# Conditioning of the second norm's scale: nine blocks in three bf16 parts, seven of them split on GpSimd

## The chip, the core and the metric

The kernel runs on one core of a Trainium2 chip. Five engines matter here. TensorE (PE in the profile; its weight loads are PEld) multiplies matrices. VectorE (DVE), ScalarE (ACT) and GpSimd (POOL) do the element work. SyncE (SP) issues most of the DMAs; the POOL queue issues some. The metric is the device time of one execution in microseconds.

## The reference, cut to what matters

One step of a one-layer decoder runs over 288 tokens: 256 of a prompt and 8 samples of 4 tokens. Nine conditioning vectors, one for the prompt and one per sample, give six modulation rows through one large weight:

```python
mod = (jax.nn.silu(c) @ w_ada + b_ada).reshape(n, N_MOD, 1, D_MODEL)
sh_m, sc_m, gt_m, sh_f, sc_f, gt_f = [mod[:, i] for i in range(N_MOD)]
...
h2 = _rms(x, g_ffn) * (1 + sc_f) + sh_f
gate, up = jnp.split(h2 @ w_ffn_in, 2, axis=-1)
x = x + gt_f * ((jax.nn.silu(gate) * up) @ w_ffn_out)
```

The change is about `sc_f`, the scale of the second norm: nine rows of 2048 values that must be there before `h2` is made. Everything is float32.

## The kernel before

**The main stream.** All large products run as steps on PE. A step loads a 1 MB block of weights by one SP DMA into one of five `raw` buffers. ACT copies each segment of 512 columns to a rounded upper part (`hi`), DVE subtracts to get the rest (`lo`), and PE multiplies three times for every 128 columns (L575 to L577: upper by upper, upper by rest, rest by upper), each with 288 columns moving. `hi` and `lo` have four buffers each (SPB), so ACT may begin the next segment only when PE has finished the one four segments back. This order of ACT, DVE and PE repeats through the whole kernel.

**The list of steps around the change** is `d0 + wo`, numbered from 0. Steps 0 to 35 are projections (`wD`), 36 to 43 the product `pa`, 44 to 51 the product `pb`, 52 to 67 the product `wo`, which adds to `x` and collects the squares for the second norm. Each of the steps 36 to 67 holds 48 matmuls. `beside[i]` lists what is put in after step i. Then come four blocks `fk`, which begin the FFN with the not yet normed `x` times the scale, and the long FFN stream (`ff`).

**The conditioning.** `w_ada` is cut into units; unit `a4` is `sc_f`, unit `a5` is `gt_f`. Each has 16 blocks of 128 rows by four groups of 512 columns. The nine columns of silu(c) lie in `cs`, padded to 32, and are the stationary operand; the weights move. The four groups of 512 run on four groups of 32 array columns (`tile_position`). There are two forms:

- Class `Ada` (L423) multiplies the float32 block as it is loaded. All 16 blocks of `a4` use it, eight after step 47 and eight after step 57. In each eight, four blocks arrive as eight pieces of 256 columns in the shared `slot` pool (`apart`, by the function `eight`), the rest in `raw`. All are loaded by SP.
- Class `Thirds` is used by all 16 blocks of `a5`. ACT casts the block to bf16 (`cast`), DVE subtracts twice in place (`cut`), and so the block becomes three bf16 parts whose sum is the float32 value. PE multiplies each part with a stationary operand that holds silu(c) in three bf16 parts of nine columns (`csr`), and `fin` adds the three. A block that is `lent` sits in 12 tiles of the `slot` pool and is handled in pieces of 256 columns, else in the pool `thirds` in pieces of 1024. The POOL queue loads both kinds (L594, L599). For `a5`, `prepared` places loads, casts, cuts and products by a written plan.

After the last block of `a4`, `tail` copies the sum out of PSUM, PE transposes it, and DVE adds the bias into `mod`. The sink of `wo` block 8 makes `gm2` from it, and from there on `scaled` (L312) makes two of the sixteen operands of `fk` per step, with small GpSimd operations.

**Order.** DVE, ACT and SP are no longer held to program order in this part. PE is held by `S["pe"]` up to step 52, where `strict` is switched off. A planner places the instructions of each engine by its own costs. Two blocks are split early and kept: `fk[3]` in the pool `short` and the first `ff` block in `slot`, at steps 60 and 61. `change` closes the pool `short` and opens `thirds` in its place, after `fk`.

Of the kernel before, what the change touches and what calls it, by code (L numbers as in the profile page):

```python
# [89 lines left out]
def _body(tc, nc, d, pc, pw, pslot, pshort, reopen, ptmp, pps):  # L90
    ids = [0]

    def nm(s):
        ids[0] += 1
        return f"{s}_{ids[0]}"
# [16 lines left out]
    def behind(i):  # L112
        return tc.issue_after(i.ins) if i is not None else ExitStack()
# [17 lines left out]
    V, A, G, PE, SY = Pinned(nc.vector), Pinned(nc.scalar), nc.gpsimd, nc.tensor, Pinned(nc.sync)  # L131
# [34 lines left out]
    cs = cs9[:, NC:].rearrange("p (k i) -> p k i", i=32)  # L166
# [7 lines left out]
    def part16(a, i):  # L174
        return a.bitcast(BF16).rearrange("p (n b) -> p b n", b=2)[:, i, :]
# [1 line left out]
    def change():  # L177
        S["thirds"] = reopen()

    def thirds_columns():  # L180
        c = tmp(16 * NC)
        cv = c.rearrange("p (k i) -> p k i", i=NC)
        r = S["csr"] = pc.tile([P, 16, 32], BF16, tag="cs", name="csr", padded_shape=[P, 16, 64])
        V.tensor_scalar(cv, ctt, 0.5, None, ALU.mult)
        for i in range(3):
            ri = r[:, :, NC * i : NC * i + NC]
            V.tensor_copy(ri, cv)
            if i < 2:
                V.tensor_tensor(cv, cv, ri, ALU.subtract)
        V.tensor_scalar(  # L190
            r[:, :, 3 * NC :], ones[:, : 32 - 3 * NC].unsqueeze(1).to_broadcast([P, 16, 32 - 3 * NC]), 0.0, None, ALU.mult
        )
# [104 lines left out]
    def in_order(i):  # L297
        if S["strict"]:
            S["pe"] = i
        return i  # L300
# [79 lines left out]
    class Step:  # L380
        defer = False
        after, lead = None, 0
        raw = None
        parts = None
# [104 lines left out]
    class Blk(Step):  # L489
# [55 lines left out]
                self.low()  # L545

        def keep(self):
            for c in range(0, self.nk * self.nm * P if not self.parts else 0, 256):
                raw, (hi, lo) = self.raw[:, c : c + 256], [slot(F32R, (P, 256), self.kept == "short") for _ in range(2)]
                with behind(S["high"]):  # L550
                    A.copy(hi, raw)
                V.tensor_tensor(lo, raw, hi.bitcast(F32), ALU.subtract)
                self.parts += [(hi[:, i : i + P], lo[:, i : i + P]) for i in (0, P)]
# [28 lines left out]

    class Thirds(Ada):
        lent = False

        def load(self):
            src = d[self.name][self.blk]
            self.ks = 1
            if self.lent:
                self.words = [slot(shape=(P, 256)) for _ in range(8)]  # L590
                tops = [slot(shape=(P, 256)).bitcast(BF16) for _ in range(4)]
                self.tops = [tops[i // 2][:, 256 * (i % 2) : 256 * (i % 2) + 256] for i in range(8)]
                for i, w in enumerate(self.words):
                    G.dma_start(w, src[:, 256 * i : 256 * i + 256])  # L594
                return
            raw = S["thirds"].tile([P, 2048], F32, tag="word", name=nm("word"))
            top = S["thirds"].tile([P, 2048], BF16, tag="top", name=nm("top"))
            self.words, self.tops = ([t[:, 1024 * h : 1024 * h + 1024] for h in range(2)] for t in (raw, top))
            G.dma_start(raw, src)  # L599

        def pieces(self):
            n = 2 if self.lent else 1
# [7 lines left out]
        def cut(self, piece):  # L610
            for i in piece:
                r = self.words[i]
                with behind(S["low"]):
                    V.tensor_tensor(r, r, self.tops[i], ALU.subtract)
                V.tensor_tensor(part16(r, 0), r, part16(r, 1), ALU.subtract)

        def run(self):
            if self.blk == 0:
                Ada.cur[self.name] = pps.tile([P, 512], F32, tag="ada", name=nm("ada"), bufs=1)
            acc = Ada.cur[self.name]  # L620
            n = 256 if self.lent else 512
            for p in range(3):
                parts = self.tops if p == 0 else [part16(w, 2 - p) for w in self.words]
                for h in range(512 // n):
                    for j in range(4):
                        at = 512 * j + n * h
                        w, o = parts[at // (2048 // len(parts))], at % (2048 // len(parts))
                        with behind(S.get("pe")):
                            self.last = in_order(
                                PE.matmul(  # L630
                                    acc[32 * j : 32 * j + 32, n * h : n * h + n],
                                    S["csr"][:, self.blk, :],
                                    w[:, o : o + n],
                                    start=self.blk == 0 and p == 0,
                                    stop=self.blk == 15 and p == 2,
                                    tile_position=(0, 32 * j),
                                    skip_group_check=True,
                                )
                            )
            self.words = self.tops = None  # L640
            if self.blk == 15:
                self.tail()
# [70 lines left out]

    def ada(name):
        u = units[name]
        return [(Thirds if name == "a5" else Ada)(u, b) for b in range(16 // u[3])]


    S = {"strict": True}
# [517 lines left out]
            done = max(done, want)  # L1237
        return out

    def prepared(main, unit, plan):  # L1240
        out = {i: [] for i in range(-1, len(main))}
        blks = iter(unit)
        for last, parts in plan:
            for lent, begin_, (p0, p1) in parts:
                u = next(blks)
                u.lent = lent
                out[begin_].append(Do(u.load))
                n = 4 if lent else 2
                for i in range(n):
                    k = p0 + (p1 - p0) * i // n  # L1250
                    out[k].append(Do(lambda u=u, i=i: u.cast(u.pieces()[i])))
                    out[k + 1].append(Do(lambda u=u, i=i: u.cut(u.pieces()[i])))
                out[last].append(Do(u.run))
        return sum(([s] + out[i] for i, s in enumerate(main)), out[-1])

    rh1 = h1.__getitem__
# [63 lines left out]
    steps = [Do(silu), Do(lambda: warm(10)), *aA[:2], Do(lambda: warm(1, aA[1].last)), aA[2]]  # L1320
# [15 lines left out]
    def wD(m0, m1):  # L1336
        return [Blk("wD", i, rh1, sinkD) for i in range(m0 // 2, m1 // 2)]

    d0 = wD(32, 40)
# [7 lines left out]
    wo = [Blk("wo", i, mg.__getitem__, sink_wo) for i in range(16)]  # L1347
    a2, a3, a4 = ada("a2"), ada("a3"), ada("a4")
    a2[-1].defer = True

    def late(unit):
        unit[-1].tail = unit[-1].out
        return [Do(lambda: unit[-1].fin(chained))]

    def eight(blks):
        for b in blks[1:5]:
            b.apart = True
        return blks


    def ffin(q):
        fi = [Blk("fi", i - 4, h2.__getitem__, lambda j, ps: sink_fi(j + 4, ps)) for i in range(max(4, 22 * q), 22 * q + 22)]
# [3 lines left out]
    fk[0].defer = fk[1].defer = True  # L1366
    ff = ffin(0)
    early = [fk[3], ff[0]]
    early[0].kept, early[1].kept = "short", "long"
    beside = {}  # L1370
    for i in range(8):
        beside[5 * i + 2] = []
# [1 line left out]
    for i, (a, b) in ((7, (0, 5)), (12, (5, 10)), (17, (10, 15)), (22, (15, 20)), (27, (20, 25)), (37, (25, 32))):  # L1374
        for u in aa[a + 1 : b - 3]:
            u.apart = True
        beside[i] += aa[a:b]
    beside[42], beside[47], beside[57] = [], eight(a4[:8]), eight(a4[8:])
    for i in range(4):
        beside[5 * i + 7].append(Do(v_transpose(i)))  # L1380
        beside[5 * i + 27].append(Do(spatial(i)))
# [1 line left out]
    beside[22] += [Do(s_transpose), Do(sg_load)]  # L1383
    beside[5] = [Do(v_squares)]
    beside[42][:0] = late(a3) + [Do(half_gt)]
    for i, s in enumerate(d0 + wo):
        if s is wo[0]:
            steps.append(Do(lambda: S.update(strict=False, pe=None)))
        if s in (wo[8], wo[9]):
            steps.append(Do(early[s is wo[9]].split))  # L1390
        steps += [s] + beside.pop(i, [])
    def ffout(q):
        return [Blk(f"f{q}", i, act.__getitem__, sink_fo(q)) for i in range(16)]
# [3 lines left out]
    a5 = ada("a5")  # L1397
# [1 line left out]
        nxt = ffin(q + 1)  # L1399
        ff += nxt[:2] + ffout(q) + nxt[2:]  # L1400
    out3 = ffout(3)
    steps.append(Do(change))
    plan = [
# [4 lines left out]
    ]  # L1408
    rest = prepared(ff, a5, plan)
    rest.insert(rest.index(ff[5]), Do(thirds_columns))  # L1410
    steps += rest + out3[:2] + [Do(join15)] + out3[2:] + [Do(finish)]

    AHEAD = RAW
# [4 lines left out]
    order = list(stream)  # L1418
    for s in [s for s in stream if isinstance(s, Ada) and s.apart]:
        i = order.index(s)  # L1420
        order.remove(s)
        order.insert(i - 6 + (s.blk % 8 if s in a4 else 1), s)
    for s, b in zip(early, (wo[7], wo[8])):
        order.remove(s)
        order.insert(order.index(b), s)
    for s in order:
# [14 lines left out]
    blks = [s for s in stream if isinstance(s, Blk)]  # L1441
    nxt, cur = 0, 0
    for s in steps:
# [3 lines left out]
        i = pos[id(s)]  # L1447
# [141 lines left out]
```

## Time and profile before

| | |
|---|---|
| three runs | 1513.66, 1515.87, 1517.86 us; median 1515.87 |
| the profiled execution | 1513.66 us, its span 1511.9 us |
| PE, PEld | busy 1504.7 and 1449.6 us |
| DVE, ACT, POOL | busy 1060.9, 776.5 and 176.6 us |
| granted TensorE clock | 0.999 |

The span is what the profile covers; 1.8 us lie around it. Times in a timeline are microseconds from the span's start. The pieces of one matmul row overlap, so the pace of PE is read from the starts of successive matmuls, not from their durations.

### The profile page before, as it was taken

To read this page: it belongs to the slowest core of one execution; us is meant where nothing else is said; L and a number is where in the kernel's file an instruction comes from. 1 tells how busy PE (TensorE), PEld (TensorE's weight loads), DVE (VectorE), ACT (ScalarE), POOL (GpSimd) and SP (SyncE) were. 2 spreads that over 40 slices of the span, in tenths; PEclk is the share of its full clock that TensorE was granted. 3 is DMA by queue.
4 is the path that set the end of the run, shared out by engine and by line. 5 is a ranking of instruction groups with operands and counts; after the bars stand their busy time and mean duration, and the time that the engine had idled before them with its cause. 6 is when DMAs were issued, how large, how long until landed. Compare 5 with 4: busy or idle time off the path is not lost.

```text
span 1511.9 us, 32334 instructions
## 1 busy us (share of the span) xinstructions
PE 1504.7 (100%) x12734; PEld 1449.6 (96%) x12734; DVE 1060.9 (70%) x2099; ACT 776.5 (51%) x1487; POOL 176.6 (12%) x353
## 2 busy tenths in 40 slices
PE   9999999999999999999999999999999999999998
PEld 8898999998899898989999999999999999999998
DVE  6786677978666576667878666666666567675586
ACT  5443354743345444457655455455545454454465
POOL 2555410000030000002500101100010100100000
PEclk9999999999999999999999999999999999999999
DMA  9977876578888778875654657564575745754452
GB/s 390 357 282 301 344 272 219 197 285 313 328 321 311 261 258 299 272 278 204 225 190 163 218 189 244 205 215 142 180 248 183 251 136 178 243 186 157 146 176 98
DMA packets 75689, 357.75 MB, mean 237 GB/s; under 512 B 9248, under 2 KB 28512, under 8 KB 46352
## 3 DMA queue, kind: packets, MB, share of 16 engines
q1 hardware_dynamic: 70384, 337.02, 62.4%
q0 software_dynamic: 5008, 18.59, 3.5%
q8 instruction: 99, 1.62, 0.4%
q14 instruction: 54, 0.44, 0.1%
q10 hardware_dynamic: 144, 0.07, 0.0%
HBM read 352.56 MB, written 3.09 MB: 235 GB/s over the span
## 4 chain that ended last, share of the span: by engine, by line
PE 100%; DVEq 0%; DVE 0%; issue 0%
PE pm L575 30%; PE pm L577 30%; PE pm L576 30%; PE ada L423 5%; PE ada L630 1%; PE px L304 1%; PE px L310 0%; PE pm L690 0%; PE pm L692 0%; PE pm L691 0%; PE pm L674 0%; PE px L733 0%; PE px L692 0%; PE px L691 0%; PE px L690 0%; PE pm L304 0%
## 5 line engine op out<-in xcount | busy, mean ns | idle before, releaser
L575 PE MATMUL pm<-s,hi 128*128 128x288 f32 (+1 forms) x3688 | 1058.1, 287 | 0.0
L577 PE MATMUL pm<-s,lo 128*128 128x288 f32 (+1 forms) x3688 | 1055.0, 286 | 0.0
L576 PE MATMUL pm<-s,hi 128*128 128x288 f32 (+1 forms) x3688 | 1054.9, 286 | 0.0
L124 ACT CAST hi<-raw 128x512 fp32r<-128x512 f32 (+2 forms) x956 | 578.4, 606 | 633.7 <-PE pm L576 547.1
L124 DVE TENSOR_TENSOR lo<-raw,hi 128x512 fp32r<-128x512 f32 (+2 forms) x959 | 657.2, 691 | 333.5 <-ACT hi L124 310.8
L575 PEld LDWEIGHTS pm<-s,hi 128*128 128x128 f32 x3688 | 697.0, 189 | 10.8 <-issue 8.9
L576 PEld LDWEIGHTS pm<-s,hi 128*128 128x128 f32 x3688 | 697.1, 189 | 0.0
L577 PEld LDWEIGHTS pm<-s,lo 128*128 128x128 f32 x3688 | 697.0, 189 | 0.0
L124 DVE TENSOR_TENSOR s<-pm,s 128x288 f32<-128x288 f32 x175 | 78.8, 454 | 24.8 <-PE pm L577 20.5
L594 POOL DMA_DIRECT2D s<-in_a x64 | 34.1, 538 | 344.7 <-PE pm L577 327.2
L423 PE MATMUL ada<-raw,cs 128*32 128x512 f32 (+3 forms) x640 | 61.8, 515 | 0.0
L124 ACT CAST s<-t 128x288 fp32r<-128x288 f32 (+2 forms) x109 | 50.3, 465 | 18.2 <-DVE t L124 15.4
L124 DVE TENSOR_TENSOR s<-t,s 128x288 fp32r<-128x288 f32 (+1 forms) x109 | 50.1, 462 | 10.7 <-ACT s L124 10.4
L124 DVE SCALAR_TENSOR_TENSOR t<-t,pm 128x288 f32<-128x288 f32 x84 | 37.9, 451 | 12.5 <-PE pm L577 8.5
L423 PEld LDWEIGHTS ada<-raw,cs 128*32 128x32 f32 x640 | 18.7, 112 | 25.3 <-issue 17.3
L124 DVE TENSOR_TENSOR s<-s,s 128x256 f32<-128x256 f32 (+2 forms) x96 | 38.4, 430 | 0.5 <-ACT s L124 0.5
L315 POOL TENSOR_TENSOR t<-x,gm 128x32 f32<-128x32 f32 x16 | 7.7, 483 | 262.5 <-DVE acc L124 248.4
L124 ACT CAST s<-s 128x256 bf16<-128x256 f32 (+1 forms) x80 | 29.7, 414 | 1.8 <-DVE s L124 1.8
L803 POOL TENSOR_TENSOR s<-s,rb 128x288 f32<-128x288 f32 x30 | 29.1, 991 | 0.0
L599 POOL DMA_DIRECT2D word<-in_a x8 | 4.4, 549 | 196.4 <-PE ada L630 142.8
L124 DVE SCALAR_TENSOR_TENSOR s<-pm,s 128x288 f32<-128x288 f32 x48 | 24.3, 511 | 2.5 <-PE pm L577 2.5
L124 ACT COPY s<-pm 128x288 f32<-128x288 f32 (+1 forms) x53 | 21.1, 401 | 9.1 <-PE pm L577 8.5
(189 smaller groups left out, 721.2 us busy)
## 6 DMA issues: line engine op xcount, KB each, us to landing
raw<-in_fi SPq DMA_DIRECT2D x84, 1024.0 KB, 4.9
raw<-in_f SPq DMA_DIRECT2D x64, 704.0 KB, 4.1
raw<-in_wD SPq DMA_DIRECT2D x36, 1024.0 KB, 8.3
raw<-in_a SPq DMA_DIRECT2D x32, 1024.0 KB, 5.1
raw<-in_wC SPq DMA_DIRECT2D x20, 896.0 KB, 6.1
raw<-in_aE SPq DMA_DIRECT2D x16, 1024.0 KB, 7.5
s<-in_a SPq DMA_DIRECT2D x128, 128.0 KB, 5.2
raw<-in_wo SPq DMA_DIRECT2D x16, 1024.0 KB, 6.7
```

Source lines behind the costliest of these rows:

```text
L124: i = f(*args, **kw)
L304: return in_order(op(*args, **kw))
L315: G.tensor_tensor(sam(a[:, TP:T]), sam(x[:, k, TP:]), bc4(gm[:, k, 1:]), ALU.mult)
L423: PE.matmul(acc[32 * j : 32 * j + 32, c], cs9[:, 32 * kt : 32 * kt + 32] if second else cs[:, kt, :], self.raw[2 * j + h] if self.apart el ...
L575: PE.matmul(ps[:, : self.n], wh, ah, start=first, stop=False)
L576: PE.matmul(ps[:, : self.n], wh, al, start=False, stop=False)
L577: self.last = in_order(PE.matmul(ps[:, : self.n], wl, ah, start=False, stop=last))
L594: G.dma_start(w, src[:, 256 * i : 256 * i + 256])
L599: G.dma_start(raw, src)
L630: PE.matmul(acc[32 * j : 32 * j + 32, n * h : n * h + n], S["csr"][:, self.blk, :], w[:, o : o + n], start=self.blk == 0 and p == 0, stop= ...
L803: G.tensor_tensor(a[:, :T], a[:, :T], S[rb], ALU.mult)
```

## The change

Unit `a4` is mixed. Blocks 4 to 7 and 11 to 15 are of class `Thirds`, blocks 0 to 3 and 8 to 10 stay float32 products. They add up in the same PSUM tile.

- A new function `planned`, taken out of `prepared`, places the nine blocks in the list. Blocks 4 to 7 are lent, loaded after steps 37 and 38, cast and cut after steps 39 to 45, and run after step 47 behind four float32 blocks. Blocks 11 to 15 are loaded after steps 47 and 52, cast and cut after steps 49 to 58, and run after step 59 (before, the second half ran after step 57). Three of these five are lent, two lie in `thirds`.
- The cuts of seven blocks are issued to GpSimd (`eng` is `G`), those of blocks 4 and 13 to DVE.
- Lent blocks are loaded by the POOL queue. The two others of `a4` are loaded by SP.
- No block of `a4` is `apart` any more. A second `csr` is made for `a4` after step 40.
- `change` moves to step 52; `fk[3]` is kept in two `word` tiles of `thirds`, and both early splits move by one step. `strict` ends at step 61 instead of 52.

```diff
+        if name == "a4":
+            r = slot(shape=(P, 256)).bitcast(BF16).rearrange("p (k i) -> p k i", i=32)
...
-            G.dma_start(raw, src)
+            (SY if self.name == "a4" else G).dma_start(raw, src)
...
                 with behind(S["low"]):
-                    V.tensor_tensor(r, r, self.tops[i], ALU.subtract)
-                V.tensor_tensor(part16(r, 0), r, part16(r, 1), ALU.subtract)
+                    self.eng.tensor_tensor(r, r, self.tops[i], ALU.subtract)
+                self.eng.tensor_tensor(part16(r, 0), r, part16(r, 1), ALU.subtract)
...
-        return [(Thirds if name == "a5" else Ada)(u, b) for b in range(16 // u[3])]
+        thirds = {"a4": (4, 5, 6, 7, 11, 12, 13, 14, 15), "a5": range(16)}.get(name, ())
+        return [(Thirds if b in thirds else Ada)(u, b) for b in range(16 // u[3])]
...
-    beside[42], beside[47], beside[57] = [], eight(a4[:8]), eight(a4[8:])
+    beside[42], beside[47], beside[59] = [], a4[:4], a4[8:11]
...
+    plan = [
+        (47, [(True, 37, (39, 42)), (True, 37, (39, 41), G), (True, 38, (41, 43), G), (True, 38, (43, 45), G)]),
+        (59, [(True, 47, (49, 51), G), (True, 47, (51, 53), G), (True, 52, (54, 58)), (False, 52, (53, 55), G), (False, 52, (54, 56), G)]),
+    ]
+    for i, v in planned(len(d0 + wo), [u for u in a4 if isinstance(u, Thirds)], plan).items():
+        beside[i] = beside.get(i, []) + v
+    beside[52][:0] = [Do(change)]
+    beside[40].append(Do(lambda: thirds_columns("a4")))
     for i, s in enumerate(d0 + wo):
-        if s is wo[0]:
+        if s is wo[9]:
             steps.append(Do(lambda: S.update(strict=False, pe=None)))
-        if s in (wo[8], wo[9]):
-            steps.append(Do(early[s is wo[9]].split))
+        if s in (wo[9], wo[10]):
+            steps.append(Do(early[s is wo[10]].split))
```

Each entry of a plan reads: lent or not, the step after which it is loaded, the steps over which it is cast (the cut of a piece comes one step after its cast), and the engine of the cut.

More of the change, by code (lines that the diff above doesn't have):

```diff
@@ L178, in change, with thirds_columns @@
         S["thirds"] = reopen()
-    def thirds_columns():
+    def thirds_columns(name):
+        if name == "a4":
+            r = slot(shape=(P, 256)).bitcast(BF16).rearrange("p (k i) -> p k i", i=32)
+        else:
+            r = pc.tile([P, 16, 32], BF16, tag="cs", name="csr", padded_shape=[P, 16, 64])
+        S["csr" + name] = r
         c = tmp(16 * NC)
         cv = c.rearrange("p (k i) -> p k i", i=NC)
-        r = S["csr"] = pc.tile([P, 16, 32], BF16, tag="cs", name="csr", padded_shape=[P, 16, 64])
         V.tensor_scalar(cv, ctt, 0.5, None, ALU.mult)
@@ L547, in keep @@
         def keep(self):
+            if self.kept == "words" and not self.parts:
+                words = [S["thirds"].tile([P, 2048], F32R, tag="word", name=nm("word")) for _ in range(2)]
             for c in range(0, self.nk * self.nm * P if not self.parts else 0, 256):
-                raw, (hi, lo) = self.raw[:, c : c + 256], [slot(F32R, (P, 256), self.kept == "short") for _ in range(2)]
+                raw = self.raw[:, c : c + 256]
+                if self.kept == "words":
+                    hi, lo = (w[:, c : c + 256] for w in words)
+                else:
+                    hi, lo = (slot(F32R, (P, 256)) for _ in range(2))
                 with behind(S["high"]):
@@ L584, in _body @@
         lent = False
+        eng = V
         def load(self):
@@ L631, in run @@
                                     acc[32 * j : 32 * j + 32, n * h : n * h + n],
-                                    S["csr"][:, self.blk, :],
+                                    S["csr" + self.name][:, self.blk, :],
                                     w[:, o : o + n],
@@ L1238, in weave, with planned @@
         return out
-    def prepared(main, unit, plan):
-        out = {i: [] for i in range(-1, len(main))}
+    def planned(steps, unit, plan):
+        out = {i: [] for i in range(-1, steps)}
         blks = iter(unit)
         for last, parts in plan:
-            for lent, begin_, (p0, p1) in parts:
+            for lent, begin_, (p0, p1), *eng in parts:
                 u = next(blks)
-                u.lent = lent
+                u.lent, u.eng = lent, eng[0] if eng else V
                 out[begin_].append(Do(u.load))
@@ L1253, in prepared @@
                 out[last].append(Do(u.run))
+        return out
+    def prepared(main, unit, plan):
+        out = planned(len(main), unit, plan)
         return sum(([s] + out[i] for i, s in enumerate(main)), out[-1])
@@ L1353, in late @@
         return [Do(lambda: unit[-1].fin(chained))]
[L1355 to L1358, printed above, removed]
     def ffin(q):
@@ L1368, in _body @@
     early = [fk[3], ff[0]]
-    early[0].kept, early[1].kept = "short", "long"
+    early[0].kept, early[1].kept = "words", "long"
     beside = {}
@@ L1401, in _body @@
     out3 = ffout(3)
-    steps.append(Do(change))
     plan = [
@@ L1409, in _body @@
     rest = prepared(ff, a5, plan)
-    rest.insert(rest.index(ff[5]), Do(thirds_columns))
+    rest.insert(rest.index(ff[5]), Do(lambda: thirds_columns("a5")))
     steps += rest + out3[:2] + [Do(join15)] + out3[2:] + [Do(finish)]
@@ L1421, in _body @@
         order.remove(s)
-        order.insert(i - 6 + (s.blk % 8 if s in a4 else 1), s)
-    for s, b in zip(early, (wo[7], wo[8])):
+        order.insert(i - 5, s)
+    for s, b in zip(early, (wo[8], wo[9])):
         order.remove(s)
```

## The prediction

> **What bounds the kernel now.** I read the page's first part (engines) and fourth (the chain that ended last) first, then the timeline of PE around the conditioning, then DVE and POOL by windows.
>
> ```profile
> span 1511.9 us, 32334 instructions
> PE 1504.7 (100%) x12734; PEld 1449.6 (96%) x12734; DVE 1060.9 (70%) x2099; ACT 776.5 (51%) x1487; POOL 176.6 (12%) x353
> PE 100%; DVEq 0%; DVE 0%; issue 0%
> ```
>
> PE sets the end from first to last: the chain is PE alone, and PE is not busy for only 1511.9 - 1504.7 = 7.2 us. So there is no wait in this part that the change could remove. It can win what PE computes less, and lose whatever makes PE wait.
>
> **What PE saves.** The timeline of PE shows the eight float32 blocks after step 47 and, later, four blocks of three parts of the unit `a5` (start, duration, line, operation, count). Two of those four are lent, two are not.
>
> ```profile
> 577.23 0.29 PE L576 MATMUL pm<-s,hi 128*128 128x288 f32 x1
> 577.36 0.29 PE L577 MATMUL pm<-s,lo 128*128 128x288 f32 x1
> 577.57 1.07 PE L423 MATMUL ada<-raw,cs 128*32 128x512 f32 x8
> 578.45 3.64 PE L423 MATMUL ada<-s,cs 128*32 128x256 f32 x64
> 581.91 2.76 PE L423 MATMUL ada<-raw,cs 128*32 128x512 f32 x24
> 584.60 0.39 PE L575 MATMUL pm<-s,hi 128*128 128x288 f32 x1
> ...
> 835.67 0.40 PE L630 MATMUL ada<-top,csr 128*32 128x512 bf16 x4
> 835.90 0.63 PE L630 MATMUL ada<-word,csr 128*32 128x512 bf16 x8
> 836.35 1.55 PE L630 MATMUL ada<-s,csr 128*32 128x256 bf16 x48
> 837.70 0.42 PE L630 MATMUL ada<-top,csr 128*32 128x512 bf16 x4
> 837.91 0.66 PE L630 MATMUL ada<-word,csr 128*32 128x512 bf16 x8
> 838.50 0.39 PE L575 MATMUL pm<-s,hi 128*128 128x288 f32 x1
> ```
>
> A float32 block takes (584.60 - 577.57) / 8 = 0.879 us, a block of three parts (838.50 - 835.67) / 4 = 0.708 us. Nine blocks save 9 x 0.171 = **1.54 us**. The main matmuls are 0.12 us apart (577.23, 577.36), the first conditioning matmul comes 0.21 us after the last main one. The change leaves two such groups, so this is unchanged, but inside each group PE now passes once from float32 to bf16. No row shows that. Its cost lies between 0 and the same 0.09 us of extra gap, twice; I take the middle, 0.1 us in all, since both operands go to the same tile and nothing is waited for. 48 matmuls of 288 columns at 0.1225 us make a step of 5.88 us.
>
> **What it adds elsewhere.** The pieces have prices in the trace, except the two subtractions on POOL, whose nearest row is a two-input float32 operation of the same size:
>
> ```profile
> L124 ACT CAST s<-s 128x256 bf16<-128x256 f32 x64 | 22.5, 402 | 0.0
> L124 DVE TENSOR_TENSOR s<-s,s 128x256 f32<-128x256 f32 x64 | 24.1, 419 | 0.0
> L124 DVE TENSOR_TENSOR s<-s 128x256 bf16<-128x256 f32 x64 | 25.0, 445 | 0.0
> L594 POOL DMA_DIRECT2D s<-in_a x64 | 34.1, 538 | 344.7 <-PE pm L577 327.2 <-DMA word<-in_a 15.0 <-DMA s<-in_a 1.1
> L954 POOL TENSOR_TENSOR s<-s,cp x4: 722/728/742, 418.4 to 431.1; 128x256 f32<-128x256 f32 x4
> L804 POOL TENSOR_TENSOR s<-s x48: 235/422/702, 59.9 to 183.0; 128x32 f32<-128x32 f32 x48
> ```
>
> - POOL, first group: three lent blocks, 3 x 8 pieces x 2 = 48 operations of 0.728 us = 34.9 us. It can begin after the casts of step 39 (step 47 ended at 577.4, so step 39 at 530) and must be done about when the four float32 blocks and the first part blocks are through, 577.4 + 4 x 0.879 + 1.4 = 582. So 52 us stand against 35: it fits while an operation takes less than 52 / 48 = 1.08 us. The bf16 side of the second subtraction is unknown on POOL; on DVE it costs 445 against 419 ns, so I keep 0.73, with 0.73 to 1.08 open.
> - POOL, second group: 32 operations of 0.728 us and 8 of 1024 columns. From 32 columns (0.235 us) to 256 (0.728) a column costs 2.2 ns, so 1024 take an estimated 2.4 us. Together 23.3 + 19.2 = 42.5 us over ten steps (59 us). It fits.
> - POOL's queue also issues 56 loads of 0.538 us: 32 (17.2 us) ahead of the first cut, where POOL does nothing else, and 24 (12.9 us) in the second group's 59 us, 42.5 + 12.9 = 55.4. That is tight, but a load that waits for a tile of `slot` stands in front of cuts that aren't due until step 59. What cuts miss, PE waits for there.
> - ACT: 56 casts of 0.402 us and four longer ones, some 27 us over twenty steps of 5.88 us. In the windows below ACT is busy 10.17 of 23.70 us at least, and 12.48 of 23.90 at most, so they are hidden; without that cover they would cost their 1.3 us a step.
> - DVE: two blocks, each 8 x (0.419 + 0.445) = 6.9 us, and seven small ones for the second `csr` beside them.
> - SP loses nine of its blocks' loads as they were (some in eight pieces) and gets two back; the bytes are the same.
> - The tail: the second half runs two steps later, so `mod` is ready 2 x 5.88 us later, and DVE adds eight more rows. Before, PE transposed at 651.46, DVE made `gm` at 652.63 and POOL first used it at 659.73. The sink of `wo` 8 that asks for it lies one step behind the new group, 5.9 us, and transposes, bias and `gm` took 652.63 + 0.31 - 650.62 = 2.3 us. Hidden by that step; a further 0.8 us for eight additions of 0.1 us too. What comes late next is `scaled`, which has seven more steps.
>
> ```profile
> 651.46 0.60 PE L445 MATMUL px<-ident,ev 128*128 128x128 f32 x4
> 652.63 0.31 DVE L124 SCALAR_TENSOR_TENSOR gm<-mod,cp 128x144 f32<-128x144 f32 x1
> 659.73 0.70 POOL L315 TENSOR_TENSOR t<-x,gm 128x32 f32<-128x32 f32 x1 [222.36 <-DVE acc L124]
> ```
>
> **Where it can be lost: DVE beside a busy POOL.** DVE must deliver every `lo` in time. Its room in the steps concerned, by windows (busy PE, PEld, DVE, ACT, POOL): four of `pa`, the first and second four of `pb`, six of `wo`.
>
> ```profile
> 517.30:541.00 23.70, 23.70 (x196) 23.70 (x196) 15.96 (x31) 10.17 (x18) 0.00 (x0) 1.00 0.98 351
> 553.50:577.40 23.90, 23.90 (x198) 23.90 (x196) 19.34 (x38) 12.48 (x23) 0.00 (x0) 1.00 0.77 256
> 584.80:608.20 23.40, 23.40 (x192) 23.40 (x192) 17.90 (x35) 11.47 (x21) 0.00 (x0) 1.00 0.89 326
> 608.20:643.40 35.20, 35.20 (x290) 35.20 (x288) 23.35 (x48) 17.24 (x31) 0.00 (x0) 1.00 0.79 269
> ```
>
> DVE's idle time per step of 5.88 us is 1.92 us in `pa`, 1.12 and 1.38 us in `pb`, 1.98 us in `wo`. And DVE runs ahead: `hi` begins when PE lets a buffer go and the `lo` ends 1.34 us later (554.09 to 555.43 below), while PE needs it three segments of 1.47 us after that release, 4.41 us. The lead is 3.1 us.
>
> ```profile
> 554.09 0.62 ACT L124 CAST hi<-raw 128x512 fp32r<-128x512 f32 x1 [0.85 <-PE pm L576]
> 554.74 0.69 DVE L124 TENSOR_TENSOR lo<-raw,hi 128x512 fp32r<-128x512 f32 x1
> ```
>
> The trace has one stretch where POOL works on SBUF beside this same DVE work, 98 to 183 us, and one without, 190 to 280 (rows by form, with the mean ns behind the busy time; the fourth row, from the view by source, has minimum, median and maximum of `lo` in the first stretch):
>
> ```profile
> L124 DVE TENSOR_TENSOR lo<-raw,hi 128x512 fp32r<-128x512 f32 x44 | 40.1, 912 | 24.9 <-ACT hi L124 19.5 <-PE pm L577 5.1
> L803 POOL TENSOR_TENSOR s<-s,rb 128x288 f32<-128x288 f32 x30 | 29.1, 991 | 0.0
> L804 POOL TENSOR_TENSOR s<-s 128x32 f32<-128x32 f32 x30 | 14.1, 488 | 0.0
> ...
> L124 DVE TENSOR_TENSOR lo<-raw,hi x59: 418/693/1329, 97.9 to 182.8; 128x512 fp32r<-128x512 f32 x44, 128x256 fp32r<-128x256 f32 x15
> ...
> L124 DVE TENSOR_TENSOR lo<-raw,hi 128x512 fp32r<-128x512 f32 x58 | 40.0, 690 | 11.9 <-ACT hi L124 10.1
> ```
>
> Beside POOL a `lo` took 912 ns, else 690. 44 x 0.222 = 9.8 us of DVE for 43.2 us of POOL: 0.23 us per us. For the first group that is 34.9 x 0.23 = 8.0 us. Its cover over steps 40 to 47 is 4 x 1.92 + 4 x 1.12 = 12.2 us of idle DVE, less 6.9 us for the block that DVE cuts, plus the lead of 3.1 us: 8.4 us. Just covered. For the second, 42.5 x 0.23 = 9.8 us against 2 x 1.38 + 8 x 1.98 - 6.9 + 3.1 = 14.8 us. So at this rate PE hardly waits. Since 0.4 us of margin won't sit exactly where it is needed, I charge 0.5 us.
>
> The Trainium skill, "SBUF — State Buffer", section "Who interferes with whom", has a rule that speaks against the change: a VectorE instruction with two SBUF inputs and a GpSimd instruction that reads SBUF exclude each other, and the later one is blocked until the other is done. The two rows above agree in direction (912 against 690 ns). By it the waits would grow with the share of two-input work, and the sum would be the first rival's, 1527, where the measured rate gives 1515.
>
> **Sum.** -1.54 + 0.1 + 0.5 = -0.9 us: 1513.66 (the profiled execution, span and 1.8 us around it) becomes 1512.7. That execution was 2.2 us below the median of the three runs, so against the median I expect **1515.0 us**. What a measurement of this kernel can tell from no change is about 0.3%, 4.5 us; this is inside it.
>
> **Rivals.**
>
> *POOL and DVE block each other (slower).* The stretch from 98 to 183 us has few DVE operations with two SBUF inputs besides `lo`; a `pb` step has eight (four `lo`, two sums, two rests) where a `pa` step has four, and POOL is to run with hardly a pause. At twice the rate, 0.46 us per us, the first group loses 16.1 - 8.4 = 7.7 us and the second 19.6 - 14.8 = 4.8 us: 12.5 us more, 1515.9 - 1.4 + 12.5 = 1527. If every one of the 80 short POOL operations held up a `lo` for 0.64 us (the slowest `lo` beside POOL took 1.329 us, the usual one 0.69) and the eight long ones for some 2, it would be 67 us less 23.2 of cover, 1558: the far end. It decides from 0.24 us per us on in the first group, and less where the cuts that DVE does itself stand in front of `lo` in steps 40 to 42. For it: POOL's small operations are stretched too (488 ns on average against 235 at best). Against it: casts and loads pace POOL, and the median `lo` beside POOL still took 693 ns, so most of them met nothing.
>
> *POOL comes late (slower).* If a cut takes 1.2 us, the first group needs 57.6 us and has 52, PE waits 5.6 us and the second group, with its loads, some 5: 1525. Against it: the mean of the stretched row is 991 ns for 288 columns, under 1.08.
>
> *Nothing is saved.* If bf16 after float32 costs PE a pause, or the operands come just in time, 1515.9. For it only that no row shows the passage.
>
> *Faster by more than 4.5 us.* PE has 7.2 us without work in the whole span, most of it ahead of the first blocks, so no row offers it.
>
> **How the numbers follow.** The forecast 0.47; POOL and DVE blocking each other 0.35, of which 0.03 stays inside 4.5 us; POOL late 0.09; nothing saved 0.06; faster 0.03. So faster 0.03, same 0.47 + 0.03 + 0.06 = 0.56, slower 0.32 + 0.09 = 0.41. The forecast's own range is 1511.5 to 1519. To leave out no more than 2 in 10 the range goes up to 1531, past the price of both slower rivals.
>
> **What would show it.** Blocks after step 47: 4 x 0.88 + 4 x 0.71 us without a gap in front of L630. POOL's subtractions of 256 columns under 1.08 us. `lo` between 520 and 655 us under 0.9 us on average, PE's idle time as now. A pause of PE at a `hi` matmul released by DVE would show the first rival, one at L630 released by POOL the second. I am wrong if PE loses more than 5 us between 517 and 665 us.

## The result and the profile after

The changed kernel takes 1542.94 us (median; 1542.61 to 1544.03), the kernel before 1514.95 us (1513.66 to 1517.86). The ratio is 1.0184, with a 95% interval of 1.0171 to 1.0197: the change costs 28 us. The prediction of 1515.0 us was wrong, and its range, up to 1531, did not reach the result either. In the code after, the main matmuls are L585 to L587 (before L575 to L577), the float32 products L427, the products of three parts L641, and the two subtractions of a cut on POOL L625 and L626.

First the page of the kernel after: its span, busy times, the chain that ended last, and the two groups of PE instructions that now wait (busy, mean ns, then idle time ahead of them and what ended it).

```profile
span 1542.1 us, 32698 instructions
PE 1512.7 (98%) x12790; PEld 1455.7 (94%) x12790; DVE 1110.6 (72%) x2146; ACT 794.7 (52%) x1547; POOL 295.4 (19%) x497
PE 93%; DVE 4%; DMA 1%; issue 1%; ACT 1%; DVEq 0%; ACTq 0%
L587 PE MATMUL pm<-s,lo 128*128 128x288 f32 (+1 forms) x3688 | 1059.2, 287 | 18.3 <-DVE lo L124 18.1
L585 PE MATMUL pm<-s,hi 128*128 128x288 f32 (+1 forms) x3688 | 1060.7, 288 | 1.5 <-ACT hi L124 1.5
```

The chain was PE alone; now 4% of it is DVE. PE's time without work rose from 7.2 to 1542.1 - 1512.7 = 29.4 us, by 22.2. Its busy time rose too, by 1512.7 - 1504.7 = 8.0 us, although PE has less to compute. So there are two losses to find: waits, and work that ran slower.

**The waits** come almost all from one place. The view of PE's waits between 517 and 690 us (total, times, longest):

```profile
PE pm L587 <- DVE lo L124: 17.8, 10, 6.1
PE pm L585 <- ACT hi L124: 1.5, 1, 1.5
PE ada L427 <- DMA raw<-in_a: 0.3, 1, 0.3
```

PE waits for `lo`, ten times. It never waits for a part made by POOL (L641 has no row). DVE's groups by form say why `lo` is late; first the kernel before from 517 to 655 us:

```profile
L124 DVE TENSOR_TENSOR lo<-raw,hi 128x512 fp32r<-128x512 f32 x82 | 56.7, 692 | 31.4 <-ACT hi L124 28.9
L124 DVE SCALAR_TENSOR_TENSOR s<-s,pm 128x288 f32<-128x288 f32 x28 | 12.6, 451 | 3.4 <-PE pm L577 3.4
L124 DVE TENSOR_TENSOR s<-s,s 128x288 f32<-128x288 f32 x16 | 7.2, 452 | 0.0
...
L124 DVE TENSOR_TENSOR x<-t,x 128x32 f32<-128x32 f32 x6 | 1.1, 185 | 0.0
```

Then the kernel after, from 517 to 690 us, with POOL's groups of the same stretch below:

```profile
L124 DVE TENSOR_TENSOR lo<-raw,hi 128x512 fp32r<-128x512 f32 x88 | 80.7, 933 | 16.8 <-ACT hi L124 15.9
L124 DVE SCALAR_TENSOR_TENSOR s<-s,pm 128x288 f32<-128x288 f32 x28 | 12.2, 446 | 1.4 <-PE pm L587 1.4
L124 DVE TENSOR_TENSOR s<-s 128x256 bf16<-128x256 f32 x16 | 11.8, 782 | 0.0
L124 DVE TENSOR_TENSOR s<-s,s 128x288 f32<-128x288 f32 x16 | 10.0, 626 | 0.1
L124 DVE TENSOR_TENSOR s<-s,s 128x288 fp32r<-128x288 f32 x16 | 9.7, 613 | 1.1 <-PE ada L641 1.0
L124 DVE TENSOR_TENSOR s<-s,s 128x256 f32<-128x256 f32 x16 | 9.1, 601 | 0.0
L124 DVE TENSOR_TENSOR x<-t,x 128x32 f32<-128x32 f32 x8 | 4.3, 534 | 0.0
...
L625 POOL TENSOR_TENSOR s<-s,s 128x256 f32<-128x256 f32 x40 | 38.1, 970 | 5.5 <-ACT s L124 5.4
L626 POOL TENSOR_TENSOR s<-s 128x256 bf16<-128x256 f32 x40 | 33.7, 861 | 0.1
...
L625 POOL TENSOR_TENSOR word<-word,top 128x1024 f32<-128x1024 f32 x4 | 9.6, 2398 | 0.0
L626 POOL TENSOR_TENSOR word<-word 128x1024 bf16<-128x1024 f32 x4 | 8.5, 2116 | 0.3
```

Read the two forms of 288 columns side by side. With both inputs in SBUF (`s<-s,s`) the mean went from 452 to 626 ns. With one input in SBUF and the other in PSUM (`s<-s,pm`) it stayed, 451 and 446. So DVE as a whole was not slowed; nearly all of what it lost lies in its instructions with two SBUF inputs (the second subtraction of a cut, `s<-s` in the view, has two as well: the rest and a part of the same tile). A few with one input were stretched too: the three casts for the second `csr` took 581 ns on average, against 234 where POOL cuts nothing (the run with all cuts on DVE, below), some 1 us in all. Over the six rows with two inputs, with 692, 445, 452, 452, 419 and 185 ns as their means before, DVE spent some 37 us more, beside 38.1 + 33.7 + 9.6 + 8.5 = 89.9 us of POOL's subtractions: 0.41 us per us of POOL. `lo` has 88 x (0.933 - 0.692) = 21.2 us of it, the other five rows some 16.

**The slower work** stands in the windows right behind a long wait. The columns are window, length, busy PE, PEld, DVE, ACT and POOL, the granted TensorE clock, and DMA share and GB/s. The timeline of PE over the same place follows.

```profile
659.00:666.00 7.00, 0.87 (x4) 0.65 (x5) 7.00 (x7) 2.00 (x5) 5.14 (x3) 0.55 0.14 57
666.00:670.00 4.00, 4.00 (x19) 4.00 (x19) 4.00 (x12) 0.95 (x2) 0.00 (x0) 0.52 0.29 61
670.00:676.00 6.00, 6.00 (x51) 6.00 (x51) 3.99 (x11) 3.42 (x7) 0.00 (x0) 1.00 0.44 152
```

```profile
659.10 0.29 PE L586 MATMUL pm<-s,hi 128*128 128x288 f32 x1
665.52 0.61 PE L587 MATMUL pm<-s,lo 128*128 128x288 f32 x1 [6.13 <-DVE lo L124]
665.92 0.45 PE L585 MATMUL pm<-s,hi 128*128 128x288 f32 x1
666.16 0.45 PE L586 MATMUL pm<-s,hi 128*128 128x288 f32 x1
```

After the wait the matmuls start 0.24 us apart instead of 0.12, until 669.8, and the granted clock is 0.52. PE counts as busy there, which is why the busy time rose. The same happens from 561.6 to 564.0 and from 618.7 to 621.8.

**The ledger.** Take every gap between the starts of two successive main matmuls from 517 to 690 us and subtract the usual 0.1225 us. Fifteen gaps over 0.3 us hold 22.2 us, sixty-two between 0.15 and 0.3 us hold 6.8 us: about 4.8 in the three stretches at half pace, the rest mostly the one slow start after each pause. Together 29.0 us; the same stretch before has 0.5. Less these 0.5 us and the 1.24 us that the groups became shorter (below), 27.3 us are accounted for. From the last main matmul of the step that ends at 509.75 us before and 511.14 after to one behind the stage (835.46 and 865.34), the kernel after loses 29.88 - 1.39 = 28.5 us; 1.2 us of it I can't assign.

### The profile page after: what moved, and what is told of

Same layout as the page of the kernel before. It is cut to its first block, busy times and chain, and to the rows that moved or that the text cites. A ratio compares the mean times of both kernels' runs of the same rounds, so it can differ in the third digit from the quotient of the medians.

```text
span 1542.1 us, 32698 instructions
## 1 busy us (share of the span) xinstructions
PE 1512.7 (98%) x12790; PEld 1455.7 (94%) x12790; DVE 1110.6 (72%) x2146; ACT 794.7 (52%) x1547; POOL 295.4 (19%) x497
## 4 chain that ended last, share of the span: by engine, by line
PE 93%; DVE 4%; DMA 1%; issue 1%; ACT 1%; DVEq 0%; ACTq 0%
PE pm L585 28%; PE pm L587 28%; PE pm L586 28%; PE ada L427 4%; DVE lo L124 2%; DVE s L124 1%; PE ada L641 1%; DMA raw<-in_a 1%; PE px L308 1%; DMA raw<-in_aB 0%; DVE t L124 0%; PE pm L701 0%; PE pm L703 0%; PE pm L702 0%; ACT hi L124 0%
## 5 line engine op out<-in xcount | busy, mean ns | idle before, releaser
L587 PE MATMUL pm<-s,lo 128*128 128x288 f32 (+1 forms) x3688 | 1059.2, 287 | 18.3 <-DVE lo L124 18.1
L585 PE MATMUL pm<-s,hi 128*128 128x288 f32 (+1 forms) x3688 | 1060.7, 288 | 1.5 <-ACT hi L124 1.5
L124 DVE TENSOR_TENSOR lo<-raw,hi 128x512 fp32r<-128x512 f32 (+2 forms) x959 | 677.6, 714 | 318.4 <-ACT hi L124 303.2
L587 PEld LDWEIGHTS pm<-s,lo 128*128 128x128 f32 x3688 | 699.1, 190 | 21.5 <-DVE lo L124 21.3
L585 PEld LDWEIGHTS pm<-s,hi 128*128 128x128 f32 x3688 | 699.2, 190 | 11.7 <-issue 8.2
L605 POOL DMA_DIRECT2D s<-in_a x120 | 64.9, 545 | 444.9 <-PE pm L587 388.1
L427 PE MATMUL ada<-raw,cs 128*32 128x512 f32 (+3 forms) x632 | 60.9, 510 | 2.0 <-DVE cs L124 0.9
L124 ACT CAST s<-s 128x256 bf16<-128x256 f32 (+1 forms) x136 | 47.9, 409 | 24.3 <-DVE s L124 18.8
L124 DVE TENSOR_TENSOR s<-s,s 128x256 f32<-128x256 f32 (+2 forms) x112 | 52.9, 502 | 1.2 <-PE ada L641 1.0
L124 DVE SCALAR_TENSOR_TENSOR t<-t,pm 128x288 f32<-128x288 f32 x84 | 37.9, 451 | 12.5 <-PE pm L587 8.7
L427 PEld LDWEIGHTS ada<-raw,cs 128*32 128x32 f32 x632 | 17.9, 109 | 28.3 <-issue 16.9
L625 POOL TENSOR_TENSOR s<-s,s 128x256 f32<-128x256 f32 x40 | 38.1, 970 | 5.5 <-ACT s L124 5.4
L124 DVE TENSOR_TENSOR s<-s 128x256 bf16<-128x256 f32 x80 | 36.7, 512 | 0.0
L626 POOL TENSOR_TENSOR s<-s 128x256 bf16<-128x256 f32 x40 | 33.7, 861 | 0.1
```

The lines of the kernel that those rows point to most:

```text
L124: i = f(*args, **kw)
L427: PE.matmul(acc[32 * j : 32 * j + 32, c], cs9[:, 32 * kt : 32 * kt + 32] if second else cs[:, kt, :], self.raw[2 * j + h] if self.apart el ...
L585: PE.matmul(ps[:, : self.n], wh, ah, start=first, stop=False)
L587: self.last = in_order(PE.matmul(ps[:, : self.n], wl, ah, start=False, stop=last))
L625: self.eng.tensor_tensor(r, r, self.tops[i], ALU.subtract)
L626: self.eng.tensor_tensor(part16(r, 0), r, part16(r, 1), ALU.subtract)
```

## The experiments

All are edits of the kernel after. Times are medians beside the kernel before on the same chip (1514.1 to 1514.2 us). The planner places the instructions of each edited kernel anew, so an edit can also move what it doesn't name. In the runs with DVE's blocks uncut, with none cut and with three blocks it made the second `csr` 12 to 14 us earlier than in the kernel after.

**POOL writes, but does not read.** Each POOL subtraction becomes POOL memsets of the same tile, for about as much POOL time.

```diff
+                if self.eng is G:
+                    for _ in range(2 if self.lent else 4):
+                        G.memset(r, 0.0)
+                    for _ in range(2 if self.lent else 4):
+                        G.memset(part16(r, 0), 0.0)
+                    continue
```

> The changed kernel, but each subtraction on GpSimd is replaced by GpSimd memsets of the same tile (two for a piece of 256 columns, four for one of 1024), which write and read nothing. So the seven blocks lose their lower parts; the order, the casts, the loads, the products and DVE's own cuts stay, and POOL is still busy for some 0.6 us per piece and subtraction. Theory A (POOL's reads of SBUF and DVE's instructions with two SBUF inputs exclude each other, and that makes lo late): the waits of PE on lo go from 18 us to under 5 us and the time to 1514 to 1521 us. Theory B (DVE's own added work, the cuts of two blocks and the second csr in its fixed queue, makes lo late): the time stays at 1538 to 1544 us.

Measured: 1514.68 us, ratio 1.0006 (0.9996 to 1.0015). POOL's memsets took 27.0 + 22.4 + 19.9 + 15.1 = 84.4 us, nearly the 89.9 us of the subtractions; two of their groups from 517 to 665 us, and `lo` from 517 to 662 us:

```profile
L628 POOL MEMSET s<- 128x256 bf16 x80 | 27.0, 414 | 0.0
...
L626 POOL MEMSET s<- 128x256 f32 x80 | 22.4, 332 | 4.8 <-ACT s L124 4.8
```

```profile
L124 DVE TENSOR_TENSOR lo<-raw,hi 128x512 fp32r<-128x512 f32 x88 | 59.6, 688 | 23.3 <-ACT hi L124 21.6
```

`lo` is back at 688 ns, and in that stretch PE waits for no `lo`. The whole loss is gone while POOL is as busy, the loads, the casts, the float32 blocks and the three-part products stand where they stood, and DVE still cuts its two blocks. Nor is the order of DVE's queue a rival: from 511 to 645 us in the kernel after DVE runs the same 189 instructions in the same order in both traces, by tile and shape, and five of PE's ten waits for `lo`, 8.4 us, lie within them. So the loss is neither the casts on ACT, nor POOL's loads, nor its being busy, nor DVE's two cuts alone: POOL's subtractions must read SBUF for it to appear.

**POOL reads with one input.** The subtractions become copies in place.

```diff
+                if self.eng is G:
+                    G.tensor_copy(r, r)
+                    G.tensor_copy(part16(r, 0), part16(r, 1))
+                    continue
```

> The changed kernel, with each subtraction on GpSimd replaced by one GpSimd copy of the same tile onto itself (one SBUF input, one output; the lower parts of the seven blocks are then not right). DVE's instructions stay. Theory A, if what excludes DVE's two-input instructions is any read of SBUF by POOL: lo takes over 850 ns on average in the two groups and the time is 1530 to 1545 us. If it takes two inputs on POOL: lo stays at 690 ns and the time at 1514 to 1517 us, as with the memsets.

Measured: 1519.73 us, ratio 1.0038 (1.0025 to 1.0052). POOL from 517 to 690 us, `lo` from 517 to 665 us, and the waits of PE:

```profile
L625 POOL COPY s<-s 128x256 f32<-128x256 f32 x40 | 25.5, 661 | 6.2 <-ACT s L124 6.2
L626 POOL COPY s<-s 128x256 bf16<-128x256 bf16 x40 | 24.6, 653 | 0.1
```

```profile
L124 DVE TENSOR_TENSOR lo<-raw,hi 128x512 fp32r<-128x512 f32 x86 | 68.3, 809 | 16.1 <-ACT hi L124 15.2
```

```profile
PE pm L587 <- DVE lo L124: 3.9, 6, 1.7
```

One read on POOL is enough to hold DVE up: 809 against 688 ns. But the time lies below the 1530 to 1545 that I had expected. With the copies of 1024 columns POOL worked 61.6 us, two thirds of 89.9, and the loss was 5.6 us, a fifth of 28.0. Two things can explain it. Per us of POOL `lo` lost less, 86 x 0.121 / 61.6 = 0.17 us against 0.24. And the loss need not go in proportion to what DVE loses: its first part falls on DVE's idle time, and only the rest stops PE. How much each made up was not tried.

**No POOL: all nine blocks are cut by DVE.**

```diff
-        (47, [(True, 37, (39, 42)), (True, 37, (39, 41), G), (True, 38, (41, 43), G), (True, 38, (43, 45), G)]),
-        (59, [(True, 47, (49, 51), G), (True, 47, (51, 53), G), (True, 52, (54, 58)), (False, 52, (53, 55), G), (False, 52, (54, 56), G)]),
+        (47, [(True, 37, (39, 42)), (True, 37, (39, 41)), (True, 38, (41, 43)), (True, 38, (43, 45))]),
+        (59, [(True, 47, (49, 51)), (True, 47, (51, 53)), (True, 52, (54, 58)), (False, 52, (53, 55)), (False, 52, (54, 56))]),
```

> The changed kernel with all nine blocks cut by DVE, none by GpSimd, at the same places of the plan. It adds 7 x 6.9 = 48 us to DVE and takes 90 us of POOL's reads away. Theory A: lo operations keep their 0.69 us and the time falls below the changed kernel's, to 1520 to 1535 us, because DVE's added 62 us stand against some 35 us of idle time and lead in the two groups. Theory B: more of what hurts, so slower than the changed kernel, 1550 to 1570 us.

Measured: 1531.61 us, ratio 1.0115 (1.0100 to 1.0130). PE's waits in the whole run, then DVE from 517 to 690 us:

```profile
PE pm L587 <- DVE lo L124: 12.4, 7, 5.2
```

```profile
L124 DVE TENSOR_TENSOR lo<-raw,hi 128x512 fp32r<-128x512 f32 x92 | 60.4, 690 | 14.2 <-ACT hi L124 13.3
L124 DVE TENSOR_TENSOR s<-s 128x256 bf16<-128x256 f32 x56 | 22.4, 446 | 0.0
L124 DVE TENSOR_TENSOR s<-s,s 128x256 f32<-128x256 f32 x56 | 21.4, 420 | 0.0
```

Every DVE instruction has its usual time, and PE still waits, now because DVE simply has more to do: 17.4 us lost. That is less than the 28.0 us with POOL's help: seven blocks given to POOL cost more than the same seven done by the engine they were to relieve.

**DVE's two blocks are not cut** (their upper parts are multiplied three times); POOL cuts its seven.

```diff
+        uncut = property(lambda self: self.name == "a4" and self.eng is V)
...
+                if self.uncut:
+                    continue
...
-                parts = self.tops if p == 0 else [part16(w, 2 - p) for w in self.words]
+                parts = self.tops if p == 0 or self.uncut else [part16(w, 2 - p) for w in self.words]
```

> The changed kernel without the two cuts that DVE does itself: blocks 4 and 13 are cast but not cut, and their bf16 tops are multiplied three times, so PE's work is the same and these two blocks are wrong. POOL's seven blocks stay. Theory A: the waits on lo fall by what 14 us of DVE work cost beside a busy POOL, to 1530 to 1540 us; most of the loss stays. Theory B: most of the loss goes, 1515 to 1525 us.

Measured: 1531.21 us, ratio 1.0111 (1.0096 to 1.0127); `lo` 932 ns as in the kernel after, PE's waits for `lo` down from 18.1 to 7.0 us, and the wait of 5.2 us at 555.7 gone. So POOL's subtractions alone cost 17 us and DVE's two cuts another 11 on top of them, while the same two cuts cost nothing beside POOL's memsets. The two draw on the same idle time of DVE. The 11 us are not the cuts' alone, though: the second `csr` was made earlier too (its first cast at 539.2 us, 552.4 in the kernel after), and so it no longer stands where the wait of 5.2 us was.

**The long POOL subtractions in pieces of 256 columns.**

```diff
+                if self.eng is G and not self.lent:
+                    for c in range(0, 1024, 256):
+                        rc = r[:, c : c + 256]
+                        G.tensor_tensor(rc, rc, self.tops[i][:, c : c + 256], ALU.subtract)
+                        G.tensor_tensor(part16(rc, 0), rc, part16(rc, 1), ALU.subtract)
+                    continue
```

> The changed kernel with the two blocks that lie in the pool of 1024 columns cut on GpSimd in pieces of 256, four instructions for one. POOL's work is the same or 2 us more, only no single instruction lasts 2.2 us. Theory A in the form that a held-up DVE instruction waits for the length of the POOL instruction in front of it: the loss of 14 us between 647 and 670 us falls by half or more, time 1533 to 1538 us. If it is POOL's sum that counts and not the length of one instruction, 1541 to 1545 us. Theory B: no change, 1541 to 1545 us.

Measured: 1535.37 us, ratio 1.0135 (1.0120 to 1.0150); PE's waits for `lo` 14.4 us, and the wait of 6.1 us at 659 is split into shorter ones with no half pace behind them. The two blocks now take 15.2 + 15.1 = 30.3 us of POOL instead of 18.1, and yet some 7 us come back (28.0 lost before the edit, 21.2 with it). DVE's order is the same as in the kernel after up to 667 us. So it counts how long one POOL instruction lasts, not only how long they last in all.

**No block is cut at all** (all nine multiply their upper parts three times), so only PE's part of the change is left, with the loads and casts:

```diff
+        uncut = property(lambda self: self.name == "a4")
```

> The changed kernel with no cut at all: the nine blocks are loaded and cast, their bf16 tops are multiplied three times, so PE, ACT, loads and order stay and the lower parts of nine blocks are missing. This shows what the products alone are worth. Theory A: 1.5 to 1.7 us less PE work in the two groups and nothing to pay for, 1512 to 1514 us where the kernel before gives 1514 to 1515. Rival: the order of the steps, the second csr or the later end of the conditioning cost something too; then at or above the kernel before, 1515 to 1517 us.

Measured: 1514.41 us, ratio 1.0003 (0.9994 to 1.0011). The two groups take 6.40 and 6.18 us, against 7.24 us each before. The time lies between the two ranges. The saving is there on the spot, 1.9 us, but the whole does not show it. 1.6 us of that profile lie ahead of everything that was changed: the main matmul that precedes this stage starts at 509.75 us before, at 511.39 here. From there to one behind the stage (835.46 and 836.45) the run is 0.65 us shorter, because small gaps of PE take back most of the rest: by the count of the ledger they hold 1.5 us from 517 to 690 us, 0.5 before. So in these two profiles, with no cut at all, about a third of what the products save gets through.

**The version that the trace allows.** Only blocks 4, 14 and 15 in three parts, cut by DVE, whose idle time can hold them; nothing on POOL.

```diff
-        thirds = {"a4": (4, 5, 6, 7, 11, 12, 13, 14, 15), "a5": range(16)}.get(name, ())
+        thirds = {"a4": (4, 14, 15), "a5": range(16)}.get(name, ())
...
+        (47, [(True, 37, (39, 45))]),
+        (59, [(False, 52, (53, 57)), (False, 52, (54, 58))]),
```

> A smaller form of the change: only blocks 4, 14 and 15 in three parts, all cut by DVE and spread over steps 40 to 46 and 54 to 58; the other thirteen stay float32 products, seven of them loaded as pieces as in the kernel before. DVE gets 3 x 6.9 us in steps that leave it 1.1 to 2.0 us each, POOL none. Theory A: lo at 690 ns, PE waits under 1 us, PE saves 3 x 0.17 us, so 1513.5 to 1515, not to be told from the kernel before. Theory B, that any cut in DVE's queue delays lo: 1518 to 1522 us.

Measured: 1514.91 us, ratio 1.0006 (0.9997 to 1.0015); no wait for `lo`, groups of 7.06 and 6.85 us. The loss is gone, and the 0.57 us that the groups save can't be told from nothing, as expected. No version beat the kernel before by what can be measured.

## Why the prediction was wrong, point by point

**What PE saves: right.** The groups in the timeline of PE after:

```profile
589.08 0.29 PE L587 MATMUL pm<-s,lo 128*128 128x288 f32 x1
589.29 2.78 PE L427 MATMUL ada<-raw,cs 128*32 128x512 f32 x24
592.33 1.07 PE L427 MATMUL ada<-raw,cs 128*32 128x512 f32 x8 [0.25 <-DMA raw<-in_a]
593.21 2.88 PE L641 MATMUL ada<-s,s 128*32 128x256 bf16 x96
596.02 0.39 PE L585 MATMUL pm<-s,hi 128*128 128x288 f32 x1
```

From 589.08 to 596.02 are 6.94 us, the second group took 6.30; before, 577.36 to 584.60 and its like were 7.24 each. That is 0.30 + 0.94 = 1.24 us of the 1.54 forecast, and the missing part is the load at 592.33, which came a little late. Beside POOL's memsets, where PE waited for no `lo`, the groups took 6.51 and 6.31: 1.66 us saved. The passage from float32 to bf16, priced at 0.1 us, costs nothing that can be seen: 593.21 - 592.33 = 0.88 us for the last float32 block, the 0.879 of the others.

**POOL's time: longer than forecast, within its limit, and POOL was never late.** The short subtractions took 970 and 861 ns (0.73 forecast, with 1.08 as the limit), the long ones 2.40 and 2.12 us (2.4 forecast): 89.9 us in all where 34.9 + 42.5 = 77.4 were forecast. The rival "POOL comes late" falls: no wait at L641. So do the worries over the tail, ACT and the POOL queue's loads, of which the memset run keeps every one.

**DVE beside a busy POOL: the step that failed.** It charged 0.5 us, from 0.23 us of DVE per us of POOL against a cover of 8.4 and 14.8 us. Three things in it were wrong.

What it counted. The 0.23 is what `lo` loses, and for `lo` it held: 21.2 us beside 89.9 us of POOL are 0.24. (It was read a little low. With the 15 `lo` of 256 columns of that same stretch, 568 ns there and 418 alone, it would have been (9.8 + 2.3) / 43.2 = 0.28.) But the stretch from 98 to 183 us has no other DVE instruction with two SBUF inputs. The steps of the change have sums, rests and DVE's own cuts besides; the prediction's sum let these keep their usual time and gave no reason; only its first rival named the sums and rests. They lost the other 16 us, 8.3 of them in DVE's own cuts alone, and the rate was 0.41. The sign that was set up, `lo` under 0.9 us on average between 520 and 655 us, came out at 988 ns.

The cover. By the prediction's own formula, with the measured 43.9 us of POOL in the first group (48 at 0.915) and 47.4 in the second (32 at 0.915, and 18.1), 0.41 gives 18.0 - 8.4 = 9.6 and 19.4 - 14.8 = 4.6 us: 14.2 us of waiting. PE waited 22.2 us by the gaps, and the other way round: 8.0 us up to the first group and 14.2 after it, mostly between 647 and 666, where POOL's long subtractions stand in one stretch. Idle time of DVE averaged over a whole group covers a steady loss; it doesn't cover 5 us or more without a finished `lo`. A `lo` can be late by about the lead, 3.1 us, before PE stops. Such stretches come in two kinds. Timelines of DVE and POOL after show the first, one `lo` that is held (start, duration):

```profile
612.24 5.20 DVE L124 TENSOR_TENSOR lo<-raw,hi 128x512 fp32r<-128x512 f32 x1 [0.19 <-ACT hi L124]
...
612.04 1.32 POOL L625 TENSOR_TENSOR s<-s,s 128x256 f32<-128x256 f32 x2
613.31 1.18 POOL L626 TENSOR_TENSOR s<-s 128x256 bf16<-128x256 f32 x2
614.45 1.29 POOL L625 TENSOR_TENSOR s<-s,s 128x256 f32<-128x256 f32 x2
615.71 1.18 POOL L626 TENSOR_TENSOR s<-s 128x256 bf16<-128x256 f32 x2
```

A `lo` that takes 0.69 us alone starts 0.2 us behind POOL and ends at 617.4, when POOL has done all eight of its subtractions, at 0.62 us each. PE stops from 615.4 to 617.5 for it.

The two longest waits are of the second kind: other DVE instructions stand between two `lo` in DVE's queue, and POOL stretches these. Before the wait that ends at 561.2, DVE works without a pause from 552.3 to 560.1 on the second `csr`, its own cuts and what the kernel before has there too; beside the memsets the same instructions take 549.0 to 554.4, and PE doesn't wait. Before the wait that ends at 665.5 stand four subtractions of block 13:

```profile
657.76 2.44 DVE L124 TENSOR_TENSOR s<-s,s 128x256 f32<-128x256 f32 x2
660.13 4.39 DVE L124 TENSOR_TENSOR s<-s 128x256 bf16<-128x256 f32 x2
```

Beside the last two works POOL:

```profile
659.89 2.30 POOL L625 TENSOR_TENSOR word<-word,top 128x1024 f32<-128x1024 f32 x1
662.27 1.96 POOL L626 TENSOR_TENSOR word<-word 128x1024 bf16<-128x1024 f32 x1
```

DVE's four take 6.7 us where 2 x (0.419 + 0.445) = 1.7 are usual: each but the first ends just after one of POOL's long subtractions.

The pace after a wait. It was not in the sum at all: 6.8 us, of which some 4.8 ran at a granted clock of 0.52 to 0.66.

**The first rival was the right case, priced too low.** "POOL and DVE block each other" named the mechanism, and its sign came: PE pauses at L587, released by DVE. Its rate of 0.46 is close to the measured 0.41. It gave 12.5 us of loss where the kernel lost some 29, for two of the reasons above, cover taken as an average and no price for the half pace. The third it had right: it pointed at the sums and rests that the measured stretch lacks. It had a chance of 0.35; the argument against it, "the median `lo` beside POOL still took 693 ns", looked at a stretch where POOL was busy for 46 of 85 us (here its subtractions alone took 90 of 122), and a median says nothing of the few long holds that stop PE.

The rule that the prediction cited against itself, the Trainium skill, "SBUF — State Buffer", section "Who interferes with whom", also says that a GpSimd instruction that only writes doesn't contend with a VectorE instruction of two SBUF inputs. The memset run agrees (`lo` at 688 ns). It describes the loser as blocked until the other's instruction is done; the 5.20 us above show a loser blocked through eight instructions in a row.

## What to carry to other kernels

Before moving two-input work from DVE to POOL, ask whether POOL's instructions read SBUF while DVE has instructions with two SBUF inputs on the path, and count all of these, not only the ones that the critical engine waits for: here each us of POOL took 0.41 us from DVE, 0.24 from `lo`, and seven blocks given to POOL cost some 11 us more than cutting them on DVE. Compare the longest stretch without a finished `lo`, not the average loss, with the lead that the critical engine has. And a long wait of TensorE can cost more than its length: here the half pace behind three waits cost 4.8 us.

## What the runs showed of the hardware that was not expected

- The two engines do not always take turns: a `lo` waited through eight POOL subtractions (5.20 us). The other way round, two POOL subtractions took 3.73 us from 541.84 on, while DVE went through four `lo` in 2.49 us. Around 660 us (above) they do alternate.
- A POOL copy with one input in SBUF holds DVE up as well (`lo` 809 ns).
- A DVE instruction with one SBUF input can take longer beside POOL too: 581 against 234 ns for the three casts, and one `TENSOR_SCALAR` took 1084 ns beside POOL's memsets, which only write (236 in the kernel before). That it was the memsets that held it was not tried.
- TensorE's half pace comes after pauses that are long, but its bound is not sharp. In the kernel after and the experiments, the pauses from 3.04 us on (3.04, 3.55, 5.47 to 5.49 and 6.42, as gaps between starts) were all followed by matmuls 0.24 us apart, those up to 2.03 us not, and of those between some were (2.13 at 615.36 after, 2.24 with DVE's blocks uncut; the slow matmuls began 1.2 to 1.3 us after PE had resumed) and some not (2.37 and 2.48 with short pieces, 2.95 without POOL). The Trainium skill, "TensorE: Matmul & The Clock Gate", section "Part 1: The HAM clock gate (the "warmup" mystery)", has the clock halved after an idle window of about 3.4 us, in windows that run freely. The slow stretches of the kernel after, 2.4 to 3.9 us, are near that length; that a pause of 2.13 us can be enough is what this trace shows. What decides between two pauses of like length was not tried.
